# Six of sixteen double units of a first channel-mix product, per layer, made in seven products

## The chip, the cores and the metric

The kernel runs on one core of one Trainium2 chip. The metric is the device time of one execution in microseconds, the median of several runs.

## What is computed

A trunk of two layers works on 512 frames of width 1024. Each layer norms x, makes a wide projection of it, runs two recurrences (an mLSTM memory and a retention), merges them into x, and then does what this case is about, the channel mix:

```python
h2 = rmsnorm(x, norm2_g[i])
x = x + jnp.square(jax.nn.relu(h2 @ w_ff1[i] + b_ff1[i])) @ w_ff2[i] + b_ff2[i]
h3 = rmsnorm(x, norm3_g[i])
x = x + jax.nn.sigmoid(h3 @ w_pe_gate[i]) * (p[i] @ w_pe[i])
```

`w_ff1` is 1024 by 4096 and `w_ff2` is 4096 by 1024, all in float32.

## The kernel before

**Precision.** Every operand of a product is kept as two parts, a rounded high part (`h`) and the rest (`l`). A product is three matmuls, high by high, high by low and low by high (`mm3`, lines 450-453). ScalarE makes the high part, VectorE the rest (`split`, lines 286-288). That holds for weights too: they come from DRAM by SyncE's queue into raw tiles `wr` and are split into `wh` and `wl` on the chip (`prep_next`, from line 398). There are four raw tiles, and three buffers for split pieces of 1024 columns, so a piece is split when an earlier one has been used up.

**Units.** The work is a list of units (`unit_list`, line 152), whose weights are loaded and split in the list's order.
- A `T8` unit, or single unit, makes 128 output columns: 8 blocks of 128 by 128 weights, 24 matmuls with 512 columns (all frames) moving (`t8`, line 455). It loads 512 KB and has one piece.
- A `PAIR` unit makes 256 output columns from 2 by 2 blocks, in seven products instead of eight (`run_pair`, line 482). Each product is 12 matmuls with 256 columns moving, 84 in all. Its weights come in the pieces A, C and B (two blocks each of 256 KB loaded for A and C, one for B) and the half piece D. One block each of A and C is a sum of blocks, made in DRAM beforehand by DMAs that GpSimd issues; two more sums are made by VectorE from raw tiles (lines 430 and 433). On the activations' side sums of operand quarters are needed as well.
- The seven products run in the order P1, P5 (piece A), P6, P2 (B), P3, P7 (C), and P4 (D). P1, P6, P7 and P4 add up in one bank of PSUM, P5 and P3 in another, P2 has a third. A result is read out before the next product is added to its bank. P4 is put off: `later` keeps it, and `flush` runs it inside the next unit, behind P5 of a PAIR, behind the fourth block of a T8, or behind the second tile of an embedding unit.

Where the units of a stage use PAIR for an ordinary projection (retention's queries and keys, gates), `pair_tiles` (line 556) takes the results out: P1, P5, P6 and P4 are copied by ScalarE, P2, P3 and P7 added by VectorE, with a raised priority. `sevenfold` and `operand_sums` (lines 596 and 607) supply the operand's sums.

**The pace of the sums.** The sums in DRAM are a list of steps in the order of `groups` (line 128). An account (`tick`, line 345) is credited per unit and debited per step, and each step waits for the matmul at which it was issued. Loads of a sum are issued only after its steps.

**The channel mix.** The hidden width of 4096 is worked in four columns of 1024 (b = 0 to 3), of four tiles each (p = 0 to 3). A tile of the first product, `ff1(b, p)` (line 1387), is a double unit: two T8 units. VectorE scales each result by the norm's factor, ScalarE adds the bias, takes relu and squares it. Then `pair_quarters` and `pair_operand` split the tile's quarters and their sums (seven quarters in all, tiles `hid`), the operand of the second product. The second product, `ff2(b, p)` (line 1415), is a PAIR for every p and wants all four hidden tiles of its column. The order (`ff_order`, line 79) is: the four tiles of column 0, then for each b the tile (b+1, 0), the second product's four units of column b, and the tiles (b+1, 1) to (b+1, 3). After (3, 3) come the first embedding unit (`embed(0)`), the second product's units of column 3 and the second embedding unit.

The Tile framework orders each engine's instructions by priority and by its own estimate of when they are ready; the priority follows the order in which they are written.

Of the kernel before, what the change touches and what calls it, by code (L numbers as in the profile page):

```python
# [35 lines left out]
F32 = mybir.dt.float32  # L36
F32R = mybir.dt.float32r
AF = mybir.ActivationFunctionType
OP = mybir.AluOpType
# [3 lines left out]
P = 128  # L43
T = 512
NT = T // P
D = 1024
KT = D // P
L = 2
# [3 lines left out]
S = 256  # L52
# [9 lines left out]
SIGN = (1.0, -1.0)  # L62
# [16 lines left out]
def ff_order():  # L79

    seq = [("f", 0, p) for p in range(4)]
    for b in range(3):
# [4 lines left out]

PRODUCTS = {"P1": ("A", 0, 0), "P5": ("A", 1, 4), "P2": ("B", 0, 2), "P6": ("B", 1, 5), "P3": ("C", 0, 6),  # L90
            "P7": ("C", 1, 3), "P4": ("D", 0, 1)}

# [35 lines left out]
def groups():  # L128


    g = {}
    for i in range(L):
        def rqk(h):
            return [("w_in", 0, c + k * 256) for k in (h, h + 1) for c in (CRQ, CRK)]

        def rg(h):
            return [("w_in", 0, CRG + h * 512 + 256 * p) for p in range(4)]

        g[i, "rv0"] = [("w_in", 0, CRV)]
        g[i, "rqk0"] = rqk(0)  # L140
        g[i, "gm"] = [("w_in", 0, CGM + 256 * p) for p in (2, 3)]
        g[i, "rg0"] = rg(0)
        g[i, "rv2"] = [("w_in", 0, CRV + 1024)]
        g[i, "rqk2"] = rqk(2)
        g[i, "rg2"] = rg(2)
        g[i, "gr"] = [("w_in", 0, CGR + 256 * p) for p in range(4)]
        for b in range(4):
            g[i, f"ff{b}"] = [("w_ff2", b * 1024, 256 * p) for p in range(4)]
    return g


def unit_list(i):

    u = [("IF",)]

    def t8(w, col, row=0):
        u.append(("T8", w, row, col))

    def v(col):
        for k in range(4):  # L160
            u.append(("V", k, col))

    def pair(g, p):
        u.append(("PAIR", (i, g), p))

    def mqk(h):
        for d in range(2):
            t8("w_in", CQ + h * 256 + d * P)
        for d in range(2):
            t8("w_in", CK + h * 256 + d * P)  # L170

    def mo(h):
        for d in range(2):
            t8("w_in", CO + h * 256 + d * P)

    def rqk(h):
        for a in range(2):
            pair(f"rqk{h // 2 * 2}", h % 2 * 2 + a)

    def rg(h):  # L180
        for a in range(2):
            pair(f"rg{h // 2 * 2}", h % 2 * 2 + a)

    def full(w, col=0, row=0, lo=0, hi=8):
        for c in range(lo, hi):
            t8(w, col + c * P, row)

    mqk(0)
    v(CV)
    full("w_in", CGM, 0, 0, 2)  # L190
    mqk(1)
    mo(0)
    full("w_in", CGM, 0, 2, 3)
    mqk(2)
    mo(1)
    v(CV + 512)
    mqk(3)
    mo(2)
    full("w_in", CGM, 0, 3, 4)
    mo(3)  # L200
    u.append(("WIDE", (i, "rv0"), 0))
    full("w_bm", 0, 0, 0, 4)
    rqk(0)
    for p in (2, 3):
        pair("gm", p - 2)
        full("w_bm", 0, 0, 2 * p, 2 * p + 2)
    rqk(1)
    rg(0)
    u.append(("WIDE", (i, "rv2"), 0))
    rqk(2)  # L210
    rg(1)
    rqk(3)
    full("w_br")
    rg(2)
    rg(3)
    for p in range(4):
        pair("gr", p)
        full("w_br", 0, 1024, 2 * p, 2 * p + 2)
    full("w_out")

    def pairs(seq):
        for kind, b, p in seq:
            if kind == "f":
                t8("w_ff1", b * 1024 + 256 * p)
                t8("w_ff1", b * 1024 + 256 * p + P)
            else:
                pair(f"ff{b}", p)

    pairs(ff_order()[0])
    u.append(("PE", 0))  # L230
    pairs(ff_order()[1])
    u.append(("PE", 1))
    full("w_pe_gate")
    return u


def build(ctx, tc, ins, out):
    nc = tc.nc
    ve, ac, gp, te = nc.vector, nc.scalar, nc.gpsimd, nc.tensor
# [6 lines left out]
    def phase(name, side, bufs=1):  # L246
        return tc.alloc_tile_pool(name=name, bufs=bufs, side=side, reuse_waits="tile")
# [9 lines left out]
    cur = {}  # L257
# [197 lines left out]
    def t8(act, name):  # L455

        _, wh, wl = unit("T8")
        o = ps(name)
        for k in range(KT):
            s = slice(k * P, (k + 1) * P)  # L460
            mm3(o, wh[:, s], wl[:, s], act[0][k], act[1][k], k == 0, k == KT - 1)
            if k == 3:
                flush()
                pace()
        return o
# [119 lines left out]
    def pair_operand(name, st, hi, lo):  # L585

        v = st.rearrange("p (q t) -> p q t", t=S)
        ve.tensor_tensor(v[:, 4:6, :], v[:, 1:3, :], v[:, 0:1, :].to_broadcast([P, 2, S]), OP.subtract)
        ve.scalar_tensor_tensor(v[:, 6, :], v[:, 5, :], -1.0, v[:, 1, :], OP.mult, OP.subtract)
        ve.scalar_tensor_tensor(v[:, 7, :], v[:, 6, :], -1.0, v[:, 3, :], OP.mult, OP.subtract)  # L590
        split(st[:, 4 * S:8 * S], hi[:, 3 * S:7 * S], lo[:, 3 * S:7 * S])

    def pair_quarters(st, hi, lo):
        split(st[:, S:4 * S], hi[:, 0:3 * S], lo[:, 0:3 * S])

    def operand_sums(name, t, hi, lo, u=None):

        u = u or [tmp(f"{name}u{a}") for a in range(2)]
        a, b = slice(0, S), slice(S, T)
        ve.tensor_tensor(u[0][:, a], t[0][:, b], t[0][:, a], OP.subtract)  # L600
        ve.tensor_tensor(u[0][:, b], t[1][:, a], t[0][:, a], OP.subtract)
        ve.scalar_tensor_tensor(u[1][:, a], u[0][:, b], -1.0, t[0][:, b], OP.mult, OP.subtract)
        ve.scalar_tensor_tensor(u[1][:, b], u[1][:, a], -1.0, t[1][:, b], OP.mult, OP.subtract)
        for a in range(2):
            split(u[a], hi[a], lo[a])

    def sevenfold(act, sums):

        def parts(k):
            def get(j):  # L610
                if j < 3:
                    a, c = ((2 * k, 1), (2 * k + 1, 0), (2 * k + 1, 1))[j]
                    return [t[a][:, c * S:(c + 1) * S] for t in act]
                a, c = 2 * k + (j - 3) // 2, (j - 3) % 2
                return [t[a][:, c * S:(c + 1) * S] for t in sums]

            return get

        return [parts(k) for k in range(4)]
# [106 lines left out]
    def bcol(i, n, k):  # L726
        o, _ = _B[n]
        return bc[:, i, o + k:o + k + 1]
# [184 lines left out]
    def big(name, dt):  # L913

        return [bpool.tile([P, T], dt, name=f"{name}{k}", tag="big", bufs=KT) for k in range(KT)]
# [23 lines left out]
    for i in range(L):  # L939
        act_side, ph_side = ("right", "left") if i == 0 else ("left", "right")  # L940
# [8 lines left out]
        t = tmp(f"l{i}selraw")  # L949
# [28 lines left out]
        for k in range(KT):  # L978
            s = slice(k * P, (k + 1) * P)
            f, e = k == 0, k == KT - 1  # L980
# [245 lines left out]
        for d in range(4):  # L1226
            o = t8(xa, f"l{i}m0z{d}") if d else oz
# [7 lines left out]
            a = (f"l{i}m0{d}", 8 * (d // 2) + d % 2, qk[2 * (d // 2)][d % 2], qk[2 * (d // 2) + 1][d % 2], d < 2, n1)  # L1235
# [86 lines left out]
        for c in range(KT):  # L1322
            o = t8(yr, f"l{i}br0{c}")
            t = tmp(f"l{i}brs{c}")
# [58 lines left out]
        shift(cur["ff"], ph_side, True)  # L1383
        cur["ntmp"] = 2
        hid = {}

        def ff1(b, p):

            nm = f"l{i}f{b}{p}"
            hid[b, p] = [cur["ff"].tile([P, 7 * S], F32R, name=f"l{i}h{a}{b}{p}", tag=f"h{a}", bufs=5) for a in "hl"]  # L1390
            st = cur["ff"].tile([P, 8 * S], F32, name=nm + "st", tag="st", bufs=2)

            def evac(d, o):
                a = st[:, d * T:(d + 1) * T]
                ve.tensor_tensor(a, o, n2.b, OP.mult)
                ac.activation(a, a, AF.Relu, bias=bcol(i, "bf1", 8 * b + 2 * p + d))
                ac.activation(a, a, AF.Square)

            o = t8(n2.act, f"{nm}0")
            if b == 0 and p == 0:  # L1400
                n2.finish()
                o1 = t8(n2.act, f"{nm}1")
                n2.spread()
                evac(0, o)
                evac(1, o1)
            else:
                evac(0, o)
                evac(1, t8(n2.act, f"{nm}1"))
            pair_quarters(st, *hid[b, p])
            pair_operand(nm, st, *hid[b, p])  # L1410
# [39 lines left out]
        for kind, b, p in first:  # L1450
            if kind == "o":
                ff2(b, p)
                continue
            if (b, p) == (3, 1):
                pth, ptl = [cur["ff"].tile([P, 2, T], F32R, name=f"l{i}pt{a}", tag=f"h{a}", bufs=5) for a in "hl"]
                for k in range(2):
                    t = tmp(f"l{i}ptr{k}")
                    nc.scalar.dma_start(t, ins["pT"][i, k])
                    split(t, pth[:, k, :], ptl[:, k, :])
            ff1(b, p)  # L1460
        n2_pool.release()
        n3_pool = phase(f"n3{i}", act_side)
        n3 = Norm(f"l{i}n3", i, "g3", acts(n3_pool, f"l{i}n3"))
# [235 lines left out]
```

## Time and profile before

| | us |
|---|---|
| median of 3 runs | 2336.89 |
| lowest, highest | 2335.52, 2338.47 |
| the profiled execution's own time | 2338.24 |
| its span | 2336.5 |
| TensorE busy in it | 2317.7 |
| VectorE busy | 1722.3 |
| ScalarE busy | 1224.1 |
| GpSimd busy | 401.4 |

The span is the time from the first to the last instruction of the profiled execution. Busy times are unions of the instructions' own times. In the rows, PE is TensorE, PEld its weight loads, DVE is VectorE, ACT is ScalarE, POOL is GpSimd and SP is SyncE. A timeline row gives start, length, engine, line, operation, output and inputs, shapes and, in brackets, how long the engine had been idle and what ended that. Names begin with the layer: `l0f` is layer 0's first product, `l0o12a` bank a of its second product's unit (1, 2), `l0gr1` a gate unit made by `pair_tiles`.

### The profile page before, as it was taken

Reading aid. Unit: us, or ns where it says so; the run is one execution under the profiler, and the core shown is the slowest. Engines: PE = TensorE matmul, PEld = TensorE weight load, DVE = VectorE, ACT = ScalarE, POOL = GpSimd, SP = SyncE. Lnnn points to the kernel's source line nnn. Section 1 sums busy time; section 2 is a strip of 40 time slices with the busy share of each in tenths; the row PEclk is TensorE's granted clock in tenths of the full one; section 3 lists DMA queues with packets and bytes.
Section 4 is the critical chain, followed back from the end, with each engine's and each line's share of the span. In section 5 each row is a group of like instructions: output and inputs, shape, how many; then the busy total and the mean of one; then the engine's idle time right before and its main releaser. Section 6 shows DMA issues by size and latency. Waiting matters only on the chain.

```text
span 2336.5 us, 35728 instructions
## 1 busy us (share of the span) xinstructions
PE 2317.7 (99%) x13664; PEld 2055.3 (88%) x13664; DVE 1722.3 (74%) x2658; ACT 1224.1 (52%) x1771; POOL 401.4 (17%) x618
## 2 busy tenths in 40 slices
PE   9999999999999999999999999999999999999998
PEld 8888898898998898899888888998989988998997
DVE  7878767896665577678778777778957656776785
ACT  6756544554554445445557564454636445445464
POOL 3122212112114212112422221000000020000012
PEclk9999999999999999999999999999999999999999
DMA  6665886668688777777766666434443442333431
GB/s 214 166 172 155 249 230 183 195 176 224 176 239 253 197 205 191 206 203 189 212 177 172 154 178 196 145 121 151 129 138 114 157 154 99 127 109 94 136 122 55
DMA packets 150540, 394.95 MB, mean 169 GB/s; under 512 B 19344, under 2 KB 22800, under 8 KB 150368
## 3 DMA queue, kind: packets, MB, share of 16 engines
q1 hardware_dynamic: 99808, 247.50, 32.6%
q0 software_dynamic: 35152, 117.73, 22.9%
q10 hardware_dynamic: 15408, 27.43, 3.5%
q8 instruction: 107, 1.75, 0.3%
q14 instruction: 65, 0.53, 0.1%
HBM read 373.71 MB, written 123.73 MB: 213 GB/s over the span
## 4 chain that ended last, share of the span: by engine, by line
PE 84%; issue 6%; DVE 5%; DMA 2%; ACT 2%; POOL 1%; SPq 0%; ACTq 0%; DVEq 0%; POOLq 0%
PE l1f L451 2%; PE l0f L451 2%; PE l0f L452 2%; PE l1f L452 2%; PE l1f L453 2%; PE l0f L453 2%; PE l1br L451 1%; PE l0br L451 1%; PE l0br L453 1%; PE l1br L452 1%; PE l0br L452 1%; PE l1br L453 1%; PE l0pg L451 1%; PE l0pg L453 1%; PE l1bm L451 1%
## 5 line engine op out<-in xcount | busy, mean ns | idle before, releaser
L287 ACT ACTIVATE wh<-wr 128x1024 fp32r<-128x1024 f32 (+1 forms) x223 | 231.2, 1044 | 286.4 <-issue 62.9
L288 DVE TENSOR_TENSOR wl<-wr,wh 128x1024 fp32r<-128x1024 f32 (+1 forms) x221 | 272.4, 1234 | 73.7 <-ACT wh L287 73.5
L287 ACT ACTIVATE wh_B<-wr 128x1024 fp32r<-128x1024 f32 x100 | 105.9, 1059 | 149.8 <-PE l1bm L452 13.1
L288 DVE TENSOR_TENSOR wl_B<-wr,wh_B 128x1024 fp32r<-128x1024 f32 x100 | 122.0, 1220 | 20.8 <-ACT wh_B L287 20.8
L287 ACT ACTIVATE wh_C<-wr 128x1024 fp32r<-128x1024 f32 x76 | 80.3, 1057 | 64.4 <-issue 9.6
L287 ACT ACTIVATE wh_D<-wr 128x512 fp32r<-128x512 f32 x76 | 48.0, 631 | 124.8 <-DVE wr L433 57.2
L288 DVE TENSOR_TENSOR wl_A<-wr,wh_A 128x1024 fp32r<-128x1024 f32 x76 | 92.8, 1221 | 20.2 <-ACT wh_A L287 20.2
L288 DVE TENSOR_TENSOR wl_C<-wr,wh_C 128x1024 fp32r<-128x1024 f32 x76 | 94.3, 1241 | 16.1 <-ACT wh_C L287 15.7
L287 ACT ACTIVATE wh_A<-wr 128x1024 fp32r<-128x1024 f32 x76 | 80.0, 1052 | 47.2 <-PE l0f L452 6.7
L451 PE MATMUL l1f<-l1n2h,wh 128*128 128x512 f32 x256 | 99.9, 390 | 0.0
L451 PE MATMUL l0f<-l0n2h,wh 128*128 128x512 f32 x256 | 99.8, 390 | 0.0
L453 PE MATMUL l0f<-l0n2h,wl 128*128 128x512 f32 x256 | 99.7, 389 | 0.0
L453 PE MATMUL l1f<-l1n2h,wl 128*128 128x512 f32 x256 | 99.7, 389 | 0.0
L452 PE MATMUL l0f<-l0n2l,wh 128*128 128x512 f32 x256 | 99.6, 389 | 0.0
L452 PE MATMUL l1f<-l1n2l,wh 128*128 128x512 f32 x256 | 99.6, 389 | 0.0
L288 DVE TENSOR_TENSOR wl_D<-wr,wh_D 128x512 fp32r<-128x512 f32 x76 | 52.5, 690 | 36.9 <-ACT wh_D L287 35.8
L662 POOL TENSOR_TENSOR l1n3sum<-l1n3sum,l1n3sq 128x512 f32<-128x512 f32 x6 | 9.2, 1539 | 330.8 <-ACT l1n3sum L654 309.8
L430 DVE TENSOR_TENSOR wr<-wr,wr 128x512 f32<-128x512 f32 x76 | 52.2, 687 | 16.2 <-DMA wr<-wpairs 15.3
L453 PEld LDWEIGHTS l1f<-l1n2h,wl 128*128 128x128 f32 x256 | 48.0, 188 | 10.1
L453 PEld LDWEIGHTS l0f<-l0n2h,wl 128*128 128x128 f32 x256 | 48.0, 188 | 10.0
L452 PEld LDWEIGHTS l0f<-l0n2l,wh 128*128 128x128 f32 x256 | 48.1, 188 | 9.9
L452 PEld LDWEIGHTS l1f<-l1n2l,wh 128*128 128x128 f32 x256 | 48.1, 188 | 9.8
(5626 smaller groups left out, 8558.3 us busy)
## 6 DMA issues: line engine op xcount, KB each, us to landing
wr<-wstream SPq DMA_DIRECT2D x219, 512.0 KB, 4.5
wr<-wpairs SPq DMA_DIRECT2D x228, 256.0 KB, 3.0
wr<-wwide SPq DMA_DIRECT2D x24, 512.0 KB, 3.7
s0t<-wwide POOLq DMA_DIRECT2D x10, 512.0 KB, 5.6
s4t<-wwide POOLq DMA_DIRECT2D x10, 512.0 KB, 6.4
s12t<-wwide POOLq DMA_DIRECT2D x10, 512.0 KB, 5.4
s16t<-wwide POOLq DMA_DIRECT2D x10, 512.0 KB, 5.5
s1t<-wpairs POOLq DMA_DIRECT2D x16, 256.0 KB, 4.1
```

The lines of the kernel that those rows point to most:

```text
L287: a = ac.activation(hi_ap, src, AF.Copy)
L288: return a, ve.tensor_sub(lo_ap, src, hi_ap.bitcast(F32))
L430: ve.tensor_tensor(raws[n, "B"][:, Q:], kept.pop((n, "A"))[:, Q:], r[:, :Q], OP.add)
L451: te.matmul(o, sh, mh, start=first, stop=False)
L452: te.matmul(o, sh, ml, start=False, stop=False)
L453: cur["mm"] = te.matmul(o, sl, mh, start=False, stop=last)
L662: (add or gp).tensor_tensor(self.sum, self.sum, sq, OP.add)
```

## The change

Tiles (1, 1), (1, 3), (2, 1), (2, 3), (3, 1) and (3, 3) of the first product become PAIR units through `pair_tiles`. Their weights leave the stream of whole tiles and join the paired blocks, as groups `fp1` to `fp3` of two units each, with their sums in DRAM ahead of the second product's group of the same number. The two results are written into the tile `st` and scaled, biased, rectified and squared there as before; d = 1 comes with its sign turned, so ScalarE takes relu with scale -1.

The normed operand's sums (`ns`) are made in the first column, a quarter of them behind each tile (0, p), from tiles `n2.act`, in the tile that `ff1` uses too (tag `st`, two buffers). They live in a pool of their own, in the second layer half of them in the buffers of `big`. The other ten tiles of each layer stay double units.

```diff
+FPAIRS = ((1, 1), (1, 3), (2, 1), (2, 3), (3, 1), (3, 3))
...
         for b in range(4):
+            f = [p for c, p in FPAIRS if c == b]
+            if f:
+                g[i, f"fp{b}"] = [("w_ff1", 0, b * 1024 + 256 * p) for p in f]
             g[i, f"ff{b}"] = [("w_ff2", b * 1024, 256 * p) for p in range(4)]
...
         for kind, b, p in seq:
-            if kind == "f":
+            if (b, p) in FPAIRS and kind == "f":
+                pair(f"fp{b}", [q for c, q in FPAIRS if c == b].index(p))
+            elif kind == "f":
...
+        ns_pool = phase(f"ns{i}", act_side)
+        if i == L - 1:
+            ns = [a.bitcast(F32R) for a in big(f"l{i}nsh", F32)]
+        else:
+            ns = [ns_pool.tile([P, T], F32R, name=f"l{i}nsh{k}", tag="nh", bufs=KT) for k in range(KT)]
+        ns = ns, [ns_pool.tile([P, T], F32R, name=f"l{i}nsl{k}", tag="nl", bufs=KT) for k in range(KT)]
+        n2_seven = sevenfold(n2.act, ns)
+
+        def n2_sums(k):
+            st = cur["ff"].tile([P, 8 * S], F32, name=f"l{i}ns{k}", tag="st", bufs=2)
+            v = [st[:, a * T:(a + 1) * T] for a in range(4)]
+            for a in range(2):
+                ve.tensor_tensor(v[a], *[t[2 * k + a].bitcast(F32) for t in n2.act], OP.add)
+            operand_sums(f"l{i}ns{k}", v[:2], *[t[2 * k:2 * k + 2] for t in ns], v[2:])
...
-            def evac(d, o):
+            def evac(d, o, sign=1.0):
                 a = st[:, d * T:(d + 1) * T]
                 ve.tensor_tensor(a, o, n2.b, OP.mult)
-                ac.activation(a, a, AF.Relu, bias=bcol(i, "bf1", 8 * b + 2 * p + d))
+                ac.activation(a, a, AF.Relu, bias=bcol(i, "bf1", 8 * b + 2 * p + d), scale=sign)
                 ac.activation(a, a, AF.Square)
 
+            if (b, p) in FPAIRS:
+                def consume(y):
+                    for d in range(2):
+                        evac(d, y[d], SIGN[d])
+                    pair_quarters(st, *hid[b, p])
+                    pair_operand(nm, st, *hid[b, p])
+
+                pair_tiles(nm, n2_seven, consume, [st[:, d * T:(d + 1) * T] for d in range(2)])
+                return
...
             ff1(b, p)
+            if b == 0:
+                n2_sums(p)
+        ns_pool.release()
         n2_pool.release()
```

## The prediction

> **What bounds the kernel now.** I read the page's busy rows first, then the waits of TensorE, then single stretches of the feed-forward part.
>
> ```profile
> span 2336.5 us, 35728 instructions
> PE 2317.7 (99%) x13664; PEld 2055.3 (88%) x13664; DVE 1722.3 (74%) x2658; ACT 1224.1 (52%) x1771; POOL 401.4 (17%) x618
> ...
> PE l0o30a L503 <- DVE wl_B L288: 0.3, 1, 0.3
> ```
>
> TensorE is busy for 99% of the span, and in the feed-forward part it has no named wait over 0.3 us. Time can only be won by giving TensorE less to stream, and is lost wherever another engine now makes it wait. So I price the saved streaming first, then look for new waits.
>
> ```profile
> L451 PE MATMUL l0wo<-l0mh,wh x64: 389/389/398, 729.3 to 772.2; 128*128 128x512 f32 x64
> ...
> L453 PE MATMUL l0wo<-l0mh,wl x64: 389/389/395, 729.8 to 772.6; 128*128 128x512 f32 x64
> 847.54 0.28 PE L501 MATMUL l0o02a<-l0hh,wh_A 128*128 128x256 f32 x1
> 857.44 0.28 PE L501 MATMUL l0o03a<-l0hh,wh_A 128*128 128x256 f32 x1
> 666.58 0.28 PE L501 MATMUL l0gr1a<-l0xnh,wh_A 128*128 128x256 f32 x1
> 687.49 0.28 PE L501 MATMUL l0gr2a<-l0xnh,wh_A 128*128 128x256 f32 x1
> ```
>
> The recorded 389 ns overlap; spacing is what counts. From 729.3 to 772.6 stand 192 matmuls of 512 columns: 43.3/191 = 0.227 us each, so a single unit (24) is 5.44 and a double unit 10.88 us. Two seven-product units in a row start 9.90 us apart (857.44 - 847.54; 84 matmuls, 0.118 each). The gate stage already mixes one seven-product unit with two single ones, the new pattern exactly: its period is 687.49 - 666.58 = 20.91, so the seven-product unit costs 20.91 - 10.88 = 10.03 there.
>
> **What the change removes from TensorE.** Six units per layer, twelve in all. Those behind another seven-product unit, (b,1), save 10.88 - 9.90 = 0.98; those between single units, (b,3), save 10.88 - 10.03 = 0.85. Six of each make 11.0 us. The 9.90 is of second-product units, whose results VectorE adds up at once; the new units copy four of seven results on ScalarE, as the gate stage's do, so I lean to its figure and take 0.88 each: **-10.5 us**, with 0.85 and 0.98 as bounds.
>
> The Trainium skill ("TensorE: Matmul & The Clock Gate", section "Wait - 56ns, not 53.3ns?") gives N/2.4 GHz plus about 2.5 ns a matmul, an estimated 215.8 and 109.2 ns, so 48 x 215.8 - 84 x 109.2 = 1.19 us a unit, 14 in all. The spacings of 227 and 118 ns are both above it, the short one by more, so I don't use it.
>
> **What it adds: VectorE.** Per changed unit, weights come in three pieces and a half instead of two, with two sums of raw pieces, and three of the seven results are added from PSUM.
>
> ```profile
> L288 DVE TENSOR_TENSOR wl_B<-wr,wh_B 128x1024 fp32r<-128x1024 f32 x100 | 122.0, 1220 | 20.8 <-ACT wh_B L287 20.8
> L288 DVE TENSOR_TENSOR wl_D<-wr,wh_D 128x512 fp32r<-128x512 f32 x76 | 52.5, 690 | 36.9 <-ACT wh_D L287 35.8
> L287 ACT ACTIVATE wh_D<-wr 128x512 fp32r<-128x512 f32 x76 | 48.0, 631 | 124.8 <-DVE wr L433 57.2 <-PE l1o10a L503 3.5 <-PE l0o10a L503 3.5
> L430 DVE TENSOR_TENSOR wr<-wr,wr 128x512 f32<-128x512 f32 x76 | 52.2, 687 | 16.2 <-DMA wr<-wpairs 15.3
> L573 DVE TENSOR_TENSOR l0gr1y<-l0gr1b,l0gr1y x1: 420/420/420, 672.6 to 672.6; 128x256 f32<-128x256 f32 x1
> 785.00:829.00 44.00, 44.00 (x197) 36.45 (x196) 30.68 (x40) 27.30 (x36) 6.71 (x9) 1.00 0.78 188
> 829.00:867.00 38.00, 37.92 (x322) 37.70 (x321) 34.01 (x54) 17.45 (x20) 6.31 (x10) 1.00 0.72 211
> 776.00:785.00 9.00, 9.00 (x45) 7.53 (x45) 3.75 (x11) 1.33 (x2) 2.52 (x2) 1.00 0.63 187
> ```
>
> In the windows the third to sixth busy columns are weight load, VectorE, ScalarE and GpSimd after TensorE. One more piece 1.22, the half piece 0.69, two sums 2 x 0.69, three adds 3 x 0.42: 4.55 us of VectorE more per changed unit. A double unit now takes 30.68/4 = 7.7 of VectorE's time, so a changed one takes 12.2, against 10.0 on TensorE; with the double unit after it, 19.9 of 20.9. The sums of the normed operand (four calls in the first column of units) are each two adds of 512, four operations of 256 and two splits of 512: 4 x 0.69 + 4 x 0.42 = 4.4, 17.8 a layer. The first column has 44 - 30.7 = 13.3 idle, and 5.2 more lie free just before it (9 - 3.75), 18.5 in all: it just fits. The whole is 12 x 4.55 + 2 x 17.8 = 90 us of VectorE, hidden as long as no piece comes late. ScalarE gets a piece (1.06), the half piece (0.63) and four copies (0.38) more, 3.2 us a changed unit, on top of 27.30/4 = 6.8 per double unit: 10.0 in the 10.0 us of a changed unit but 16.8 of 20.9 with the next, so it too is hidden on the whole and can be late only locally (place one below). In the second product's units VectorE runs at 34.01 of 38 while TensorE is busy for 37.92, so close to 90% does no harm.
>
> VectorE's durations overlap:
>
> ```profile
> 860.15 0.68 DVE L433 TENSOR_TENSOR wr<-wr 128x512 f32<-128x512 f32 x1
> 860.75 0.48 DVE L1422 SCALAR_TENSOR_TENSOR l0x<-l0x,bc,l0o03c 128x256 f32<-128x256 f32 x1
> ```
>
> The next operation begins 0.60 after a start, though the first lasts 0.68. The sums above, made of durations, are therefore somewhat too high. The Trainium skill ("VectorE: DVE Perf Modes", section "Terms") says the next operation can't issue until the pipe is empty after every operation; that would leave the sums as they are and favours the slow rival below. This row goes against it, by 0.08 us an operation.
>
> **Where a wait can arise.** Three places.
>
> Place one, the start of a seven-product unit behind single ones: its third piece gets a buffer only when the unit before ends.
>
> ```profile
> 828.72 0.28 PE L501 MATMUL l0o00a<-l0hh,wh_A 128*128 128x256 f32 x1
> 831.55 0.35 PE L501 MATMUL l0o00a<-l0hh,wh_B 128*128 128x256 f32 x1
> 828.69 1.06 ACT L287 ACTIVATE wh_B<-wr 128x1024 fp32r<-128x1024 f32 x1 [2.83 <-PE l0f L452]
> 830.40 0.63 ACT L1397 ACTIVATE l0f10st<-l0f10st 128x512 f32<-128x512 f32 x1
> 831.13 0.85 ACT L287 ACTIVATE l0hh<-l0f10st 128x768 fp32r<-128x768 f32 x1
> 829.79 1.22 DVE L288 TENSOR_TENSOR wl_B<-wr,wh_B 128x1024 fp32r<-128x1024 f32 x1 [0.18 <-ACT wh_B L287]
> ```
>
> B is ready at 829.79 + 1.22 = 831.01, and its first matmul is at 831.55: 0.5 us to spare. The same product P6 also waits for ScalarE to have read P1 out of its bank. P1 ends 1.41 us after the start; if its 0.38 us copy (row L581 below) stands behind the square that ends at 831.03, P6 isn't late; if it stands behind the 0.85 us operation that follows, it ends at 831.98 + 0.38 and P6 is 0.8 us late. It has high priority, and the gate stage keeps its period with this very order, so I take 0.2 for each of six such starts: **+1.2**, bounds 0 and 6 x 0.9 = 5.4.
>
> Place two, the last unit (3,3). Its P4 is put off into the following unit, the embedding, and its hidden tile is wanted right behind that.
>
> ```profile
> 1068.73 0.40 PE L451 MATMUL l0pe<-l0pth,wh 128*128 128x512 f32 x1
> 1074.24 0.28 PE L501 MATMUL l0o30a<-l0hh,wh_A 128*128 128x256 f32 x1
> 1077.42 0.28 PE L502 MATMUL l0o30b<-l0hl,wh_B 128*128 128x256 f32 x1
> 1077.97 0.38 PE L503 MATMUL l0o30a<-l0hh,wl_B 128*128 128x256 f32 x1 [0.28 <-DVE wl_B L288]
> 1068.92 0.69 DVE L1395 TENSOR_TENSOR l0f33st<-l0f,l0n2rb 128x512 f32<-128x512 f32 x1 [2.48 <-PE l0f L453]
> 1072.34 0.96 DVE L288 TENSOR_TENSOR l0hl<-l0f33st,l0hh 128x768 fp32r<-128x768 f32 x1
> 1075.23 1.22 DVE L288 TENSOR_TENSOR l0hl<-l0f33st,l0hh 128x1024 fp32r<-128x1024 f32 x1 [1.13 <-ACT l0hh L287]
> 677.87 0.28 PE L501 MATMUL l0gr1a<-l0xnh,wh_D 128*128 128x256 f32 x1
> L581 ACT ACTIVATE l0gr1y<-l0gr1a x1: 384/384/384, 679.5 to 679.5; 128x256 f32<-128x256 f32 x1
> ```
>
> Now the scaling starts at 0.19 after the embedding's first matmul, the quarters are ready at 4.57 and the sums at 7.72 (1073.30 and 1076.45). After the change P4 begins half-way, at 2.76, its copy 1.63 later (677.87 to 679.5) for 0.38, so the scaling starts near 4.82, 4.63 later: quarters at 9.2, sums at 12.35. The first product behind it begins at 5.51 + 1.41 = 6.9 and wants the fourth hidden tile at 8.0, the second product its sums at 9.4. Kept in order, TensorE waits 1.2 and then 12.35 - 10.6 = 1.75, 3.0 in all, against 0.43 today (1077.42 to 1077.97 less one spacing). But the order can be interleaved, as the o30a and o30b rows show, and products over the first three hidden tiles fill most of it. Bounds 0.3 and 2.6 more a layer; I take 1.6: **+3.2** for two layers.
>
> Place three, the first column: the sums fit with nothing over, and o00's B has 0.5 to spare; bounds 0 and (30.7 + 17.8 - 44) = 4.5 a layer, I take 0.3: **+0.6**. The hand-over from (b,3) to the next second product has two single units between and so 9 us for a chain that ends at 12.35 - 2.76 - 1.63 = 8.0 after P4's copy begins: nothing.
>
> **DMAs.** A changed unit loads five quarter-megabytes in place of two halves, and GpSimd issues four more sums in DRAM for it.
>
> ```profile
> wr<-wpairs SPq DMA_DIRECT2D x228, 256.0 KB, 3.0
> ...
> s1t<-wpairs POOLq DMA_DIRECT2D x16, 256.0 KB, 4.1
> ```
>
> By the pacing account (lines 341-348) the new sums are issued 34 units or more ahead of use, and the tightest lead of before (8 units) lies ahead of them and stays. The loads queue on SyncE, where the second product's runs of four already have this density; with 0.72 of the DMA time used there I take nothing. Without that cover a piece would be late by up to one landing, 3.0 us.
>
> **The sum.** -10.5 + 1.2 + 3.2 + 0.6 = -5.5 us. The profiled execution took 2338.24 us (span 2336.5), 1.35 above the median 2336.89 of the runs; against the median the forecast is **2331.4 us**, with 2328 to 2335 as its own range.
>
> **Rivals.**
> - *All hidden.* The interleaved order swallows places one to three: -10.5, 2326.4 us. For it speaks the gate stage's clean period; against it place two. Chance 0.20.
> - *P1's copy behind the splits.* ScalarE works its queue in order; place one at its upper bound, +4.2 on the forecast: 2335.6 us. Chance 0.12.
> - *VectorE becomes the bound (slower).* If dependences keep VectorE from being filled beyond the 34.01/38 = 0.895 of today's densest stretch, each period of a changed unit and a double one takes 19.9/0.895 = 22.2 instead of 20.9, 1.3 lost twelve times, 15.6; the first column takes 48.5/0.895 = 54.2 against 49.2, 10 for two layers. -10.5 + 25.6 = +15.1: 2352.0 us. It decides from the fill at which the loss equals the gain: (12 x 19.9 + 2 x 48.5)/(12 x 20.9 + 2 x 49.2 + 10.5) = 0.93. For it: every double unit shows VectorE waiting for TensorE. Against: at 0.895 TensorE did not wait, so that is no proven ceiling, and over the whole stage there is slack in the second product. Chance 0.18.
>
> The forecast has 0.50. About 0.2% (4.7 us) is what a measurement of this kernel can tell from no change. Of the forecast's 0.50 I count 0.34 as faster than that and 0.16 within; with all hidden (0.20), faster is 0.54; with the copy (0.10 within, 0.02 slower) and a little of VectorE (0.02 within, 0.16 slower), within is 0.28 and slower 0.18. The range runs from 2325, under the all-hidden case, to 2344, half-way into the slow one.
>
> **What would show it.** Right: in the first product, 504 matmuls of 256 columns a layer spaced 0.118 us in place of 288 of 512 spaced 0.227, no named TensorE wait above 0.5 there but at l0o30 and l1o30, where the hold-up is 1 to 3 us; VectorE near 0.9 busy from the first column to the embedding. Wrong: waits of TensorE on wl_B or on an ACT copy at every changed unit, of a microsecond each (the copy), or VectorE without gaps and the units' spacing stretched (the bound); or o30 starting more than 3 us late.

## The result and the profile after

The changed kernel took 2349.73 us (median of 4 runs, 2346.26 to 2352.14) against 2337.68 for the kernel before: 1.0044 times as long, interval 1.0032 to 1.0055. It is about 10 us slower by this ratio and 12 by the medians; I had forecast 2331.4, in a range up to 2344.

From the changed kernel's page (busy rows, and the sums of raw pieces on VectorE) and from the waits of TensorE (engine and line, what it waited for, us in all, times, longest):

```profile
span 2350.4 us, 37031 instructions
PE 2320.1 (99%) x14096; PEld 2076.0 (88%) x14096; DVE 1789.8 (76%) x2806; ACT 1265.3 (54%) x1859; POOL 432.5 (18%) x666
...
L438 DVE TENSOR_TENSOR wr<-wr,wr 128x512 f32<-128x512 f32 x88 | 60.4, 687 | 54.4 <-DMA wr<-wpairs 48.1 <-issue 5.7
...
PE l1r0brqa L509 <- DVE l1r0brqy L587: 3.3, 1, 3.3
PE l0r0o0c L509 <- ACT l0r0o0y L579: 2.8, 1, 2.8
...
PE l0o30a L510 <- DVE l0hl L296: 0.9, 1, 0.9
...
PE l0o30b L511 <- DVE wl_B L296: 0.6, 1, 0.6
...
PE l0o30b L509 <- ACT wh_B L295: 0.6, 1, 0.6
```

VectorE rose by 67 us (1722.3 to 1789.8), less than my 90, whose durations overlap. In the third row, VectorE's sums of raw pieces, the idle time ahead of them was 16.2 us before, of which 15.3 for loads. It is now 54.4 us, of which 48.1 for loads that have not landed, and what stands behind such a sum in VectorE's queue stands still too. This row isn't the size of the loss, though. Of the 38.2 us more, 23.1 lie in the two channel mixes, where TensorE's longest wait is 0.9 us, and the row still has 49.2 us in experiment e1, which is faster. The part that goes there is that of layer 1's retention (1400 to 1600 us of each trace): 2.0 us before, 12.0 now, 1.3 in e1. Of TensorE's waits, the largest two are in the retention stage, which the change doesn't touch.

The start of each stage's first matmul, in the trace after against the trace before, tells where the time went. The profiled executions took 2352.14 and 2338.24, 13.9 apart:

| stage | after - before, us |
|---|---|
| layer 0, retention (l0r1brqa to l0r0o1a) | +3.5 |
| layer 0, channel mix (l0f to l0pg) | +2.6 |
| layer 1, retention (l1r0brqa to l1r0o1a) | +7.2 |
| layer 1, channel mix (l1f to l1pg) | +0.9 |

The channel mixes together lost 3.5 where I had forecast a gain of 5.5; 10.7 were lost in the two retention stages.

**Layer 1's retention.** Windows of the kernel before (first two rows) and after (last three); the last columns are the granted clock, the DMA engines' share and GB/s:

```profile
1440.00:1460.00 20.00, 20.00 (x90) 16.57 (x89) 10.71 (x13) 6.31 (x7) 0.00 (x0) 1.00 0.44 139
1460.00:1480.00 20.00, 20.00 (x153) 19.22 (x151) 12.43 (x17) 8.65 (x15) 0.00 (x0) 1.00 0.39 120
```

```profile
1440.00:1460.00 20.00, 20.00 (x90) 16.45 (x89) 12.03 (x15) 6.93 (x8) 5.66 (x9) 1.00 0.89 252
1460.00:1480.00 20.00, 20.00 (x128) 18.21 (x127) 9.10 (x11) 7.28 (x10) 6.88 (x11) 1.00 0.87 209
1480.00:1500.00 20.00, 16.72 (x118) 16.51 (x117) 14.47 (x21) 7.30 (x14) 7.16 (x12) 0.83 0.90 231
```

The busy columns are TensorE, weight load, VectorE, ScalarE and GpSimd. Before, GpSimd had issued its last sum by then (at 1411.7; 0.00 busy). Now 48 more steps, two for each of 24 new sums, stand in the same list, all later ones are pushed back, and the list still runs through this stage (52 steps between 1440 and 1590): the DMA engines' share goes from 0.4 to 0.9. The loads on SyncE's queue, the chain of waits, and VectorE's and TensorE's timelines there:

```profile
1474.88 0.33 SPq L395 DMA_DIRECT2D wr<-wpairs  x1
...
1475.31 7.51 DMA wr<-s17t
...
1482.68 0.69 DVE L438 TENSOR_TENSOR wr<-wr,wr 128x512 f32<-128x512 f32 x1 [5.74 <-issue]
1483.29 0.42 DVE L585 TENSOR_TENSOR l1r0brqy<-l1r0brqc,l1r0brqy 128x256 f32<-128x256 f32 x1
...
1484.76 0.42 DVE L587 TENSOR_TENSOR l1r0brqy<-l1r0brqa,l1r0brqy 128x256 f32<-128x256 f32 x1
...
1481.67 0.28 PE L511 MATMUL l1r0brkc<-l1xsh,wl_A 128*128 128x256 f32 x1
1485.23 0.58 PE L509 MATMUL l1r0brqa<-l1xnh,wh_D 128*128 128x256 f32 x1 [3.28 <-DVE l1r0brqy L587]
1485.61 0.41 PE L510 MATMUL l1r0brqa<-l1xnl,wh_D 128*128 128x256 f32 x1
1485.82 0.41 PE L511 MATMUL l1r0brqa<-l1xnh,wl_D 128*128 128x256 f32 x1
```

The load in the chain takes 7.5 us to land. The one issued just before it, at 1474.88, is the one that the sum L438 wants: VectorE stands on its semaphore until 1482.60, 7.7 us after the issue (the row itself names no releaser). The sum waits at the head of VectorE's queue, with two results of PSUM behind it (L585, L587); the put-off P4 adds to the bank that L587 reads, so TensorE waits 3.28 us. Its two last rows start 0.21 apart, not 0.12: the clock has been halved.

```profile
407.00:413.00 6.00, 6.00 (x29) 6.00 (x30) 2.22 (x6) 2.48 (x4) 0.00 (x0) 0.51 0.00 1
1485.00:1491.00 6.00, 5.77 (x27) 5.77 (x28) 4.30 (x7) 2.09 (x4) 1.60 (x2) 0.50 0.92 206
```

These windows of the changed kernel show the granted clock at 0.51 and 0.50 just behind a wait. The trace's clock records have three such stretches ahead of the end: 6.8 us from 406.0, 3.4 us from 1081.8 and 6.8 us from 1484.6; before had none. With matmuls 0.213 us apart in place of 0.118, these 17.0 us hold the work of 9.4, so up to 7.6 us are lost, more than half of the whole loss in this execution. So a stop of about 3 us was paid twice. The Trainium skill ("TensorE: Matmul & The Clock Gate", section "What's actually happening") has the clock halved after an idle window of about 3.4 us that runs free of the kernel. The stretches of 3.4 and 6.8 us agree with such a window's length; but the waits at which the two of 6.8 began, 2.80 and 3.28 us, are shorter than it, so a window that was only partly idle was enough here. A wait of 1.95 us at l0r0o0c cost no clock before.

### The profile page after: what moved, and what is told of

It reads as the page before. It is cut to its first block, busy times and chain, and to the rows that moved or that the text cites. A ratio compares the mean times of both kernels' runs of the same rounds, so it can differ in the third digit from the quotient of the medians.

```text
span 2350.4 us, 37031 instructions
## 1 busy us (share of the span) xinstructions
PE 2320.1 (99%) x14096; PEld 2076.0 (88%) x14096; DVE 1789.8 (76%) x2806; ACT 1265.3 (54%) x1859; POOL 432.5 (18%) x666
## 4 chain that ended last, share of the span: by engine, by line
PE 73%; DVE 12%; issue 8%; ACT 3%; DMA 3%; POOL 1%; DVEq 0%; SPq 0%; POOLq 0%; ACTq 0%
DMA wr<-wpairs 1%; PE l0br L459 1%; PE l1br L459 1%; PE l1br L461 1%; PE l1br L460 1%; PE l0br L460 1%; PE l0br L461 1%; DVE wl L296 1%; DVE l0hl L296 1%; DVE l1hl L296 1%; DVE wl_B L296 1%; DVE wl_C L296 1%; PE l0pg L459 1%; PE l1bm L459 1%; PE l0pg L461 1%
## 5 line engine op out<-in xcount | busy, mean ns | idle before, releaser
L295 ACT ACTIVATE wh<-wr 128x1024 fp32r<-128x1024 f32 (+1 forms) x199 | 206.0, 1043 | 214.2 <-issue 55.4
L296 DVE TENSOR_TENSOR wl<-wr,wh 128x1024 fp32r<-128x1024 f32 (+1 forms) x197 | 242.9, 1234 | 65.8 <-ACT wh L295 65.3
L438 DVE TENSOR_TENSOR wr<-wr,wr 128x512 f32<-128x512 f32 x88 | 60.4, 687 | 54.4 <-DMA wr<-wpairs 48.1
L459 PE MATMUL l1f<-l1n2h,wh 128*128 128x512 f32 x160 | 62.5, 391 | 0.0
L459 PE MATMUL l0f<-l0n2h,wh 128*128 128x512 f32 x160 | 62.5, 391 | 0.0
L460 PE MATMUL l0f<-l0n2l,wh 128*128 128x512 f32 x160 | 62.4, 390 | 0.0
L460 PE MATMUL l1f<-l1n2l,wh 128*128 128x512 f32 x160 | 62.4, 390 | 0.0
L461 PE MATMUL l0f<-l0n2h,wl 128*128 128x512 f32 x160 | 62.3, 389 | 0.0
L461 PE MATMUL l1f<-l1n2h,wl 128*128 128x512 f32 x160 | 62.3, 389 | 0.0
L441 DVE TENSOR_TENSOR wr<-wr 128x512 f32<-128x512 f32 x88 | 60.4, 686 | 1.0
L295 ACT ACTIVATE wh_t<-wr 128x1024 fp32r<-128x1024 f32 x24 | 25.5, 1064 | 34.4 <-PE l1r2va L554 5.3
```

Of the source, the lines that this page charges most:

```text
L295: a = ac.activation(hi_ap, src, AF.Copy)
L296: return a, ve.tensor_sub(lo_ap, src, hi_ap.bitcast(F32))
L438: ve.tensor_tensor(raws[n, "B"][:, Q:], kept.pop((n, "A"))[:, Q:], r[:, :Q], OP.add)
L441: ve.tensor_tensor(r[:, :Q], r[:, :Q], r[:, Q:], OP.add)
L459: te.matmul(o, sh, mh, start=first, stop=False)
L460: te.matmul(o, sh, ml, start=False, stop=False)
```

## The experiments

Eleven kernels. Ratios are to runs of the kernel before on the same chip, whose median stands in brackets where the chip changes; "before + 3.8" is a difference to that median. The last four columns are the stages' differences to the trace of before, as above, in each kernel's one profiled execution. That is one run of several: the changed kernel's first trace and e2's are the slowest of their runs, those of e3, e5 and e6 the fastest of theirs. So the columns say where a run lost time, and only the ratios say what a change is worth.

| run | median us (before) | ratio, interval | L0 ret. | L0 mix | L1 ret. | L1 mix |
|---|---|---|---|---|---|---|
| e1_no_sums | 2342.67 (2338.83) | 1.0018, 1.0009-1.0026 | -0.3 | +3.4 | -0.6 | +0.6 |
| e2_pause | 2347.50 | 1.0035, 1.0021-1.0049 | +1.9 | +7.3 | -0.6 | +2.6 |
| e3_32 | 2341.02 | 1.0010, 1.0000-1.0021 | -0.3 | -1.8 | +2.3 | -2.5 |
| e4_sums_only | 2341.68 | 1.0012, 1.0003-1.0021 | +0.1 | +1.3 | +1.6 | +0.6 |
| e5_after_again | 2348.83 (2338.55) | 1.0039, 1.0026-1.0053 | -0.3 | +1.5 | +3.9 | +1.0 |
| e6_32_pause | 2339.92 | 1.0002, 0.9994-1.0011 | -0.2 | -1.4 | -0.6 | -1.5 |
| e7_32_pause_wo | 2335.83 | 0.9984, 0.9974-0.9993 | +1.4 | -1.8 | -0.6 | -2.1 |
| e8_33_early | 2344.91 | 1.0022, 1.0012-1.0032 | +0.2 | +2.0 | +6.4 | -1.6 |
| e9_12 | 2332.82 (2337.88) | 0.9980, 0.9970-0.9989 | +0.4 | -3.6 | -0.6 | -0.8 |
| e10_eight | 2348.78 | 1.0048, 1.0036-1.0060 | -0.4 | +3.5 | -0.6 | +8.1 |
| e11_floor | 2332.33 | 0.9979, 0.9970-0.9989 | -0.3 | -2.1 | -0.6 | -5.1 |

My theory from these two traces: three separate losses, late loads through the added sums in DRAM (DMA), the hand-over of (3,3) (chain), and the operand's sums in the first column. Each is dearer where the clock halves. The rival: VectorE has too much to do, wherever it stands.

**e1: the changed kernel without the new sums in DRAM.**

```diff
         for g, v in groups().items():
+            if g[1][:2] == "fp":
+                continue
             n = 2 if is_wide(g) else len(v)
...
+        if g[1][:2] == "fp" and x not in GIVEN:
+            return given[g, "B12"]
         return given[g, x] if x in GIVEN else sums[g, x]
```

> The changed kernel with the DRAM sums of the new units left out (they load a given block in place of each sum, so their results are other numbers; loads, splits and matmuls are all there). DMA theory: the 7 us that layer 1's retention lost against before (waits of TensorE at l1r0brqa and l1r1brqa, raw loads landing late while the DMA engines were 0.87 to 1.02 busy) go away, and the time is before + 4 to + 6 us, 2342 to 2344; DMA share at 1440 to 1540 us falls back to about 0.45. VectorE theory: VectorE's work is the same, so the time stays at before + 11 to + 13.

Before + 3.8, where the changed kernel is at + 12.0 (and at + 10.3 in e5), each against its own before: the new sums in DRAM cost 6.4 to 8.2 us. Layer 1's retention is at -0.6. Its window there, and the row of VectorE's sums of raw pieces:

```profile
1460.00:1480.00 20.00, 20.00 (x135) 18.48 (x134) 11.68 (x16) 7.14 (x10) 0.00 (x0) 1.00 0.52 141
...
L442 DVE TENSOR_TENSOR wr<-wr,wr 128x512 f32<-128x512 f32 x88 | 60.4, 686 | 49.2 <-DMA wr<-wpairs 48.2 <-DVE l1r0brqy L585 0.7
```

The DMA share is back to 0.52. VectorE does the same work as in the changed kernel (busy 1788.6 us against 1789.8), so the VectorE theory fails for this part.

**e2: no sums issued during layer 1's retention.**

```diff
     def pace():
-        if at["step"] < len(steps) and at["credit"] >= 0:
+        if not 176 <= at["unit"] < 228 and at["step"] < len(steps) and at["credit"] >= 0:
             step()
 
     def tick(kind=None):
+        if 176 <= at["unit"] < 228:
+            return
```

> The changed kernel with all its sums, but none issued from unit 176 to 227 (layer 1 from just before its first wide unit up to the output projection); the rest follow in the output projection and the channel mix. DMA theory: the same gain as without the sums, before + 4 to + 6, because the channel mix of layer 1 has its DMA engines 0.3 to 0.45 busy and layer 0's at 0.8 shows no late load. VectorE theory: unchanged, before + 11 to + 13. A third possibility, that sums delay loads wherever they stand: the loss moves to layer 1's channel mix, and the time stays.

Layer 1's retention is clean again, as without the sums:

```profile
1460.00:1480.00 20.00, 20.00 (x108) 17.31 (x107) 9.15 (x11) 5.22 (x8) 0.00 (x0) 1.00 0.36 119
...
1930.00:1987.00 57.00, 57.00 (x257) 47.27 (x256) 45.21 (x76) 31.37 (x44) 18.30 (x24) 1.00 0.78 193
```

The sums now run in layer 1's channel mix (share 0.78 in its first column, without a wait of TensorE there; further on, at l1o02a, waits of 0.8 and 0.4 us are new). But the time, before + 8.7, is not clear of the changed kernel's, against my expectation. In the profiled execution layer 0's mix lost 7.3 with two stretches at half clock, though the program there is the changed kernel's, which lost 2.6 and 1.5 in its two traces. So these losses vary from run to run, and one trace doesn't say by how much; the pause alone is inconclusive in time.

**e3: (3,2) in place of (3,3).**

```diff
-FPAIRS = ((1, 1), (1, 3), (2, 1), (2, 3), (3, 1), (3, 3))
+FPAIRS = ((1, 1), (1, 3), (2, 1), (2, 3), (3, 1), (3, 2))
```

> The changed kernel with unit (3,2) in seven products in place of (3,3), so that the last tile before the embedding is a double unit again. Chain theory: the late start of the last column's second product (l0o30 and l1o30, 5.4 and 4.8 us later than the units before it would have it, of which 1.5 is the put-off P4) goes, 3 to 4 us a layer, and the time is the changed kernel's - 6 to - 8, before + 4 to + 6. VectorE theory: the same work in the same stretch, at most 1 us gained a layer, before + 10 to + 12.

Before + 2.2: the interval lies below the changed kernel's, 8.1 to 9.9 us less, each against its own before. The last column (l0o30a to l0o33a) costs +0.8 and -0.4 in the two layers; with (3,3) it was +5.4 and +3.4. What it was, in the changed kernel (TensorE, then VectorE):

```profile
1078.71 0.39 PE L510 MATMUL l0o30a<-l0hl,wh_A 128*128 128x256 f32 x1 [0.91 <-DVE l0hl L296]
1079.88 0.38 PE L509 MATMUL l0o30b<-l0hh,wh_B 128*128 128x256 f32 x1 [0.56 <-ACT wh_B L295]
...
1081.33 0.39 PE L511 MATMUL l0o30b<-l0hh,wl_B 128*128 128x256 f32 x1 [0.63 <-DVE wl_B L296]
1082.16 0.42 PE L510 MATMUL l0o30a<-l0hl,wh_B 128*128 128x256 f32 x1
1082.38 0.42 PE L511 MATMUL l0o30a<-l0hh,wl_B 128*128 128x256 f32 x1
...
1078.91 1.23 DVE L296 TENSOR_TENSOR l0hl<-l0f33st,l0hh 128x1024 fp32r<-128x1024 f32 x1 [0.26 <-ACT l0hh L295]
1080.05 1.22 DVE L296 TENSOR_TENSOR wl_B<-wr,wh_B 128x1024 fp32r<-128x1024 f32 x1
```

The embedding starts at 1068.20, so the hidden tile's sums are ready 11.9 us behind it (1080.14; I had 12.35). But B is split behind them, so TensorE waits a second and a third time, and then the clock halves (0.22 between the 1082 rows).

**e4: the operand's sums alone**, with `FPAIRS = ()`.

> The changed kernel with no unit in seven products, so that only the normed operand's sums of the first column are added to the kernel before (nobody reads them). If the first column's fill costs what the trace after shows at l0o00 to l0o03 and l1o00 to l1o03 (1.2 us a layer): before + 2 to + 3. VectorE theory, first column at 0.895 fill: before + 10. If the hitches there come from the seven-product units behind them: before + 0 to + 1.

Before + 2.9, as expected from the trace. VectorE's busy time (third) in the first column, e4 and then the changed kernel:

```profile
785.00:829.00 44.00, 44.00 (x196) 36.41 (x195) 42.21 (x68) 29.75 (x41) 6.70 (x9) 1.00 0.74 174
```

```profile
789.00:833.00 44.00, 44.00 (x198) 36.49 (x197) 43.32 (x70) 29.56 (x42) 10.43 (x16) 1.00 0.74 175
```

VectorE is filled to 96 and 98%, and TensorE still isn't held up within the column. The 1.4 and 1.0 us of the two layers come behind it, in the second product's first units (l0o00a to l0o03a, l1o00a to l1o03a), with the backlog. This trace also lost 1.6 us in layer 1's retention, with 3.4 us at half clock from 1566.2, where the kernel has nothing new; so the sums account for 2.4 of the 2.9.

**e5: the changed kernel again**, on the chip of e6 to e8.

> The changed kernel once more, so that the others of this call have it on their own chip. It was before + 12 in its first runs; the traces so far give it + 3 in the two channel mixes, + 6 in layer 1's retention from late loads and up to + 3.5 in layer 0's, of which the last two vary from run to run: before + 7 to + 13, with a wider spread than the kernel before.

Before + 10.3. Its trace has a wait of 2.2 us at l1r0brqa but no half clock in the retention stages, and layer 1's retention costs +3.9 in place of +7.2. Its only half clock ahead of the end, 3.4 us from 2240.7, lies behind l1o30.

**e6: (3,2) and the pause together**, the diffs of e2 and e3.

> Unit (3,2) in place of (3,3), and no sum issued from unit 176 to 227. If chain and DMA are separate losses, both go: in the trace of (3,2) the two channel mixes stood at - 1.8 and - 2.5 against before, and layer 1's retention at + 2; with the pause that goes to 0, so before - 3 to - 5. If the sums only move their harm into layer 1's channel mix: before - 1 to + 2. VectorE theory (its fill decides): before + 8 or more.

The profiled execution (2335.04) is as expected for two separate losses, the median isn't: before + 1.4, within the noise, and not separable from e3 either. That is in the range I had given for sums that only move their harm into layer 1's channel mix (-1 to +2). So in time the pause's worth is not shown, here or in e2. VectorE's work is that of the changed kernel, so the VectorE theory (+8 or more) fails.

**e7: the operand's sums in the output projection**, on top of e6.

```diff
             n2.tile(c, x[c])
+            if c % 2:
+                n2_sums(c // 2)
         cur["low"].release()
...
-            st = cur["ff"].tile([P, 8 * S], F32, name=f"l{i}ns{k}", tag="st", bufs=2)
-            v = [st[:, a * T:(a + 1) * T] for a in range(4)]
+            v = [tmp(f"l{i}nsr{k}{a}") for a in range(2)]
...
-            if b == 0:
-                n2_sums(p)
```

> As the run with (3,2) and the pause, with the normed operand's sums made in the output projection, where VectorE is 21.9 of 44 us busy, in place of the first column. If the sums cost 0.95 to 1.4 us a layer in the first column because they fill VectorE there, that goes and nothing comes in its place: 2 to 3 us below the run with (3,2) and the pause, before - 5 to - 8. If VectorE now holds the norm behind the output projection: at or above that run.

Faster than before by 2.7 us, less than the 5 to 8 that I expected, since e6 wasn't where its trace had put it; and 4.1 below e6, more than expected, with intervals that just don't meet.

```profile
729.00:773.00 44.00, 44.00 (x195) 36.41 (x194) 37.54 (x51) 20.51 (x29) 18.07 (x21) 1.00 0.82 214
787.00:831.00 44.00, 44.00 (x196) 36.40 (x195) 30.60 (x39) 27.27 (x35) 10.48 (x16) 1.00 0.76 191
```

VectorE has 37.5 of 44 in the output projection (21.9 before) and 30.6 in the first column, as in the kernel before; no wait takes their place.

**e8: (3,3) kept, its P4 put off less.**

```diff
-                if c == 1:
+                if c == (0 if u == 0 else 1):
                     flush()
```

> The changed kernel with (3,3)'s put-off P4 run behind the embedding unit's first tile in place of its second, 1.4 us earlier. Chain theory: l0o30 and l1o30 wait 1.4 us less each, and layer 0's short stretch at half clock behind them (1.7 us lost) may go too: 2.7 to 4.5 us below the changed kernel on the same chip. VectorE theory: no change.

3.9 us below e5, as expected, though the intervals meet. The last columns cost +3.3 and +0.8 in place of e5's +4.8 and +4.1. This trace again had the late load and the half clock in layer 1's retention (+6.4).

**e9: (1,2) and (2,2) in place of (1,3) and (2,3)**, on top of e7.

> The run with (3,2), the pause and the sums in the output projection, with (1,2) and (2,2) in place of (1,3) and (2,3): all six new units stand in a row behind the second product's. TensorE streams 0.13 us less for each of four units moved (9.90 against 10.03), 0.5 in all; VectorE gets 12 us of work a unit in three units running where it had a double unit between. Chain and DMA theory: within 2 us of that run, before - 2 to - 5. VectorE theory: each pair of new units runs into the fill, before + 2 or more.

The fastest complete kernel of this study: 0.9980 of before, 5.1 us less, near the forecast's 5.5, but with other units, the pause and the sums moved. All six new units of a layer now stand right behind the second product's units, two in a row, with no double unit between, and the VectorE theory's + 2 or more fails. Its time isn't separable from e7's. What its trace still loses, in layer 1's second product:

```profile
2014.27 0.69 DVE L440 TENSOR_TENSOR wr<-wr,wr 128x512 f32<-128x512 f32 x1 [2.58 <-DMA wr<-wpairs]
...
2015.35 0.39 PE L511 MATMUL l1o02a<-l1hh,wh_D 128*128 128x256 f32 x1 [2.02 <-DVE l1x L1458]
```

It is the late load again, at another place, with 3.4 us at half clock behind it. A wait at l1o02a stands in the trace of every kernel with both the pause and the new sums (0.6 to 1.4 us in e2, e6 and e7), and in none of the others. So the pause takes the late load out of the retention and, in e9 and e10 at least, brings one into the channel mix.

**e10: eight new units a layer**, (1,3) and (2,3) added to e9's.

> As that run, with (1,2) and (2,2) added to the six: eight new units a layer, three in a row in columns 1 and 2. If only VectorE's local fill decides, the row of three loses more than it saves, before or above. If late pieces and chains decide, four more units save 0.88 each, 3.5 us, less what the 16 further sums in DRAM cost: before - 3 to - 7.

Slower, before + 10.9: here the VectorE theory is right in part. From its waits of TensorE, two windows, the chain and VectorE's timeline:

```profile
PE l1o02a L511 <- DVE l1x L1458: 6.0, 1, 6.0
PE l1o10a L511 <- DVE l1x L1458: 1.6, 1, 1.6
...
PE l0o10a L511 <- DVE l0x L1458: 1.6, 1, 1.6
...
910.00:920.00 10.00, 8.38 (x54) 7.38 (x53) 9.73 (x16) 6.96 (x10) 0.54 (x1) 1.00 0.57 133
2008.00:2024.00 16.00, 11.16 (x95) 10.76 (x93) 7.50 (x12) 3.95 (x5) 6.21 (x9) 1.00 1.06 334
...
2015.95 8.26 DMA wr<-wpairs
...
2024.32 0.69 DVE L440 TENSOR_TENSOR wr<-wr,wr 128x512 f32<-128x512 f32 x1 [6.61 <-DMA wr<-wpairs]
```

Three new units in a row leave a wait of 1.6 us at each second product behind them, in both layers, where e9's rows of two leave none. VectorE is busy for 9.73 of the 10 us around the first of them: that is its backlog. The other 6.0 us is the late load once more, VectorE idle for 6.61 us with the DMA engines fully busy: the sums that the pause held back now collide in layer 1's mix, with a half clock behind.

**e11: e7 without the new sums in DRAM**, the diffs of e1 and e7.

> The run with (3,2), the pause and the sums in the output projection, with the new units' sums in DRAM left out (a given block is loaded in place of each sum, so their results are other numbers). DMA theory: what the sums still cost there by late loads goes, 1 to 3 us below that run, before - 4 to - 7. If the sums no longer cost anything: the same time as that run, before - 2 to - 3.

Before - 5.5, so 2.8 us below e7, each against its own before (the two ran on different chips), the intervals meeting (0.9974-0.9993 and 0.9970-0.9989); layer 1's mix is at -5.1 in place of -2.1, without a wait at l1o02a. So the sums probably still cost some 3 us in e7; by time alone that isn't shown.

## Why the prediction was wrong, step by step

- **The streaming saved**, -10.5: nearly right. Column 2's two units gain 1.58 us (l0o13a to l0o20a in the trace after; 1.68 in layer 1), 0.79 a unit where I had 0.88; 9.5 for twelve.
- **Place one**, +1.2: nothing was lost there. TensorE has no named wait in the new units in any trace but e10's (0.4 to 0.8 us in six of its sixteen).
- **Place two**, +3.2, with 2.6 a layer as the upper bound: 4.6 and 3.8, 8.4 in all (the last columns against e3's). The chain's length was right; the bound was too low because I let B's split run beside the chain, while it stood behind it on VectorE, and in layer 0 because the clock halved.
- **Place three**, +0.6: 2.4 in e4's trace. The sums did fit, but with nothing left, and the backlog came out one stage later.
- **The hand-over from (b,3)**, "nothing": the second product's units behind it (o10 to o13 and o20 to o23) took 1.0 us longer in the trace after, both layers together, and 0.8 to 2.1 in every other trace of six new units with (1,3) and (2,3), against 0.0 in e9, which has none there.
- **"I take nothing" for the DMAs**: the step that failed most. I checked that the sums come before their use, and not beside what they would now run. The list grew by 48 steps and reached into layer 1's retention, where the DMA share of before was 0.4 only because the list had ended. That the sums cost 6.4 to 8.2 us is shown in time by e1. That layer 1's retention is where they cost it shows in the stage's trace, though not in time, in e2, e6, e7 and e9. The price I gave for a late piece, 3.0 us, was the wait; that a wait of this size halves the clock for 3.4 or 6.8 us was in no row of before, and I had no term for it. Together the terms as measured, -9.5 + 8.4 + 2.4 + 1.0, make + 2.3, where e1 has + 3.8; with the 6.4 to 8.2 us that I put at nothing they come to + 8.7 to + 10.5, against the measured + 10.3 and + 12.0. Some 1.5 us are not accounted for.
- **The slow rival** came near the time (2352.0) by luck, with the wrong mechanism. VectorE can be filled to 98%, so its ceiling of 0.895 doesn't hold; e3, e6, e7 and e9 do the same work on VectorE (busy 1789.4 to 1807.7 us, against 1789.8) for 8 to 17 us less than the changed kernel, each against its own before. A local form of it holds in e10.
- Open: how much of the loss in single runs is due to layer 0's retention (+3.5 in one trace of the changed kernel, -0.3 in the other), and why e2's layer 0 lost more than the changed kernel's. Both have loads in them that land late; which transfer delays which, and whether it is in the DMA engines, in DRAM or in GpSimd's issuing, wasn't tried.

## What to carry to other kernels

When a change adds background transfers to a paced list, look up what the list's new end runs beside, not only whether each transfer comes before its use. A vector queue that works in order passes a late load on to everything behind it, the matrix engine's banks included; put the work that waits for loads where nothing urgent follows. And price a stop of the matrix engine that nears 3 us twice, since the clock may halve behind it.

## What the runs showed of the hardware

The granted clock fell to 0.5 for 3.4 or 6.8 us at or behind stops of TensorE, whose 256-column matmuls then came every 0.213 us in place of 0.118. It takes no single long stop: at l0o30 three waits of 0.91, 0.56 and 0.63 us within 4 us were followed by 3.4 us at half clock in the changed kernel, but not in e5. And waits of 2.0 us at l0r0o0c were followed by it in e7 (3.4 us from 407.8) and not in the kernel before. Over the thirteen traces of this case, each of the four waits of 2.8 us and more (2.80 and 3.28 in the changed kernel, 3.31 in e8, 6.05 in e10) went with 6.8 us at half clock; of the 28 waits of 1.5 to 2.4 us, five were followed by 3.4 us.
